# Moving VectorE work in a two-layer attention block: the gate's modulation, the query rotation, retention tiles and score maxima

## The chip, the cores and the metric

The kernel runs on one NeuronCore of a Trainium2 chip. The metric is the device time of one execution in microseconds. Five instruction streams work side by side and wait for each other through semaphores: TensorE (PE in the profile, with its weight loads as PEld), VectorE (DVE), ScalarE (ACT), GpSimd (POOL) and SyncE (SP), whose queue issues nearly all DMA transfers.

## The reference

Two layers over a sequence of 1024 tokens with 1024 features. Each layer normalizes x, scales and shifts it with a modulation computed from a condition vector c, projects it once, runs three kinds of attention on slices of that projection, gates each with a SiLU, projects back, and adds the result times a modulation gate:

```
shift, scale, gate = split(silu(c) @ ada_w[l] + ada_b[l], 3)
h = rms_norm(x, norm_w[l]) * (1 + scale) + shift
ret_p, mla_p, gla_p = split_cols(h @ w_in[l], ...)
r_o = rms_norm(retention(rope(rq), rope(rk), rv))        # 4 heads of 64, chunks of 64, decay
m_o = mla(mq, mkv, mkr, ...)                             # 8 heads, low-rank q and kv, softmax, causal by chunk
g_o = rms_norm(gla(gq, gk, gv, gg, ...)) * gla_norm      # 4 heads, gated linear attention, chunks of 64
x = x + gate * (concat(r_o*silu(rz), m_o*silu(mz), g_o*silu(gz)) @ w_out[l])
```

After two layers comes a final rms_norm. All is float32. In `mla` the queries are an up-projection of a rank-256 latent; 32 features per head are rotated by position (rope), 64 are not, and the softmax subtracts the row maximum of the scores.

## The kernel before

Features lie on the 128 partitions and tokens along the free dimension, in two halves of 512 (`hf`). A float32 product is made of three fast matmuls: each operand is split into a high and a low part, and `mm3` (L556, L557, L558) adds high by high, high by low, low by high in one PSUM bank. One projection of 128 output features over one half is 8 such triples, 24 matmuls of 128x512.

**Stages of a layer**, in PE's order: retention's queries and keys; the latents `mkv`, `mq0`, `mq1`; the retention values `rv` with features on the free side (`proj_v`, 8 groups of 128 tokens); the MLA keys (`mk`); `gq`; the rotated part of the MLA queries (`mla_queries` up to its `yield`); the gate projection `rz0`; the other MLA queries (`mla_queries` after the `yield`, tiles `mq`); `rz1`; `gk`; the values `gv` with GLA's preparation beside them; `gz0`, `gz1` with the GLA core; `mz0` to `mz3`; then the MLA heads and the output projection.

**What sets the order.** PE's order is written by hand: it is the program's order (`manual_schedule` for PE). Side work is put between the matmuls of the projections by `task` and `tick`: a task is a generator, each `tick` lowers its counter by one, and at zero one step of it is issued, which names the next distance. A projection ticks after each `mm3`, a `proj_v` after every second one. Three such tasks matter here. `ret_core` is retention tile by tile (128 tokens, 8 tiles): it starts `RW[0]` ticks after the MLA keys and spreads its tiles by `RW[1]`. `mla_max` computes 176 score tiles a layer only for their row maxima: a matmul (L1243) to a PSUM bank, and a DVE reduction (L1245) that frees it; it yields `MAXW` ticks between two of them, and its banks go round the tags in `self.maxp`. `head_out` normalizes a finished head pair, transposes it through PSUM (L874) and multiplies by the gate (L878, L880). What a task hasn't done at a `drain` is issued there at one go; the last maxima come out that way behind `mz3`, ahead of the MLA values `mv`. The orders of DVE, ACT, POOL and SP come from a scheduler with a model of time, which takes what is ready, earlier program text first; on the chip each of these engines runs its list strictly in that order.

**PSUM** has four tags of two buffers each: `pj`, `mm`, `s`, `acc`. From the MLA keys on, projections have only the two `pj` buffers, so the third one to come waits until an eviction has freed the first. Evictions are an ACT copy (L717, L1078, L694), or for the `mq` tiles an ACT copy to a high part and a DVE subtraction for the low part (`pair_out`, L1107), which frees the bank. The `s` and `mm` buffers carry retention's scores (L790, freed by DVE's decay multiplication L793), its state products (L802 freed by L804, L815 freed by L823 and L825) and the maxima.

**Modulation** (`ada`, L567-580) is no matmul: a chunk of 512 of its outputs streams 8 tiles of 256 KB through three SBUF buffers, and DVE multiplies each with a broadcast silu(c) and adds along the row (L576, 128x512 each, kept in program order). A layer's own chunks are `(l, 4)` and `(l, 5)`, the two halves of its gate, which are not used before the output projection; layer 0 also computes the four chunks of layer 1. `next_chunk(x)` is called at named points "a" to "o", and issues one chunk if x is in `CHUNKS`. Point "c" stands ahead of `proj_v` for `rv`, "e" behind `gq`, "f" behind `rz0`, "g" behind `rz1`.

**Query rotation** (`q_rope`): per half six DVE products and sums (L732 to L737) on two 128x512 tiles, two DVE casts to the high part (L1118), two POOL subtractions for the low part (L1119), and four DMAs to DRAM scratch (L1121).

## Time and profile before

| what | us |
|---|---|
| median of three runs | 1194.8 (1193.62 to 1195.11) |
| profiled execution | 1194.69 |
| its span (first to last instruction) | 1192.9 |
| PE busy | 1136.0 (95%) |
| PE weight loads busy | 947.2 (79%) |
| DVE busy | 787.9 (66%) |
| ACT busy | 595.6 (50%) |
| POOL busy | 529.5 (44%) |
| mean granted PE clock | 0.969 |

How to read it: the timeline view lists instructions of one engine with start and duration; consecutive ones of a line and shape are put together (x8), with the duration of all of them. What stands in brackets is the idle time of the engine before it, and the engine, tile and line that released it. The view by windows gives each engine's busy time in a stretch of the span, and in its column PEclk the mean granted clock of PE as a share of the full one. A `128x512` matmul starts 0.23 us after the one before it at full clock (397.19, 397.42 and 397.65 us on the timeline) and 0.43 us at half clock; its duration as listed is longer, since matmuls overlap.

### The profile page before, as it was taken

The page shows a single profiled execution, that of the slowest core. Times are in us where ns is not written, and L with a number is a line of the kernel's source. Part 1 is how long each engine was busy: PE and PEld are TensorE (multiplying, and loading weights), DVE is VectorE, ACT ScalarE, POOL GpSimd, SP SyncE. Part 2 cuts the span into 40 slices and gives each one's busy share as a digit, 9 for nine tenths or more (in the row PEclk, how much of TensorE's full clock was granted, in tenths as well). Part 3 has the DMA queues.
Part 4 walks back from the last instruction along what each step waited for, and adds up shares of the span by engine and source line. Part 5 has one row for each costly group of instructions (what it writes and reads, how often), then busy time and mean ns, then how long its engine had stood idle before and what let it go on. Part 6 is the DMA issues. An engine that isn't in the chain of part 4 may idle for free. (4 is left out here: it accounts for less than half of the span.)

```text
span 1192.9 us, 16951 instructions
## 1 busy us (share of the span) xinstructions
PE 1136.0 (95%) x5968; PEld 947.2 (79%) x5968; DVE 787.9 (66%) x1366; ACT 595.6 (50%) x1164; POOL 529.5 (44%) x459
## 2 busy tenths in 40 slices
PE   7999989899999899999999999789999989999996
PEld 4878967688877688888787898668888868888896
DVE  7864298568776656868875437863875565686754
ACT  6434432333554478863543443144355547886431
POOL 0064154245533346683565324424453334668630
PEclk8899998799999899999999999799999989999999
DMA  9816173672136634238453325536221663424722
GB/s 374 278 56 174 45 259 121 212 218 79 42 103 184 151 89 107 62 132 310 176 178 92 108 89 203 176 133 202 62 58 41 175 151 89 107 63 147 258 90 71
DMA packets 65585, 169.01 MB, mean 142 GB/s; under 512 B 10262, under 2 KB 13334, under 8 KB 65500
## 3 DMA queue, kind: packets, MB, share of 16 engines
q1 hardware_dynamic: 65500, 167.93, 45.0%
q8 instruction: 47, 0.77, 0.3%
q14 instruction: 38, 0.31, 0.1%
HBM read 125.36 MB, written 38.41 MB: 137 GB/s over the span
## 5 line engine op out<-in xcount | busy, mean ns | idle before, releaser
L457 POOL TENSOR_TENSOR wwo_wl<-wwo_wst,wwo_wh 128x1024 fp32r<-128x1024 f32 x27 | 69.1, 2563 | 38.9 <-ACT wwo_wh L456 38.9
L1269 POOL TENSOR_TENSOR mhead_wh<-mhead_p,mhead_wh 128x384 fp32r<-128x384 f32 (+1 forms) x48 | 57.9, 1206 | 56.9 <-DVE mhead_wh L1268 56.9
L576 DVE SCALAR_TENSOR_TENSOR ada_aw<-ada_aw,silrow 128x512 f32<-128x512 f32 x64 | 71.2, 1139 | 9.8 <-DMA ada_aw<-awc 9.5
L1245 DVE TENSOR_REDUCE mmax_mx<-mmax_psmm 128x1 f32<-128x512 f32 (+1 forms) x88 | 51.9, 590 | 22.0 <-PE mmax_psmm L1243 21.0
L1245 DVE TENSOR_REDUCE mmax_mx<-mmax_psacc 128x1 f32<-128x256 f32 (+2 forms) x88 | 45.5, 517 | 21.6 <-PE mmax_psacc L1243 20.4
L1274 DVE TENSOR_TENSOR mhead_ph<-mhead_pss,mhead_ph 128x512 fp32r<-128x512 f32 x48 | 33.0, 688 | 36.1 <-ACT mhead_pss L1273 36.1
L556 PE MATMUL pmz_pspj<-mkh_h,wmz_wh 128*128 128x512 f32 x128 | 52.5, 410 | 0.0
L1269 POOL TENSOR_TENSOR mhead_wl<-mhead_p,mhead_wl 128x128 fp32r<-128x128 f32 (+1 forms) x48 | 35.8, 746 | 34.8 <-DVE mhead_wl L1268 34.8
L557 PE MATMUL pmz_pspj<-mkh_h,wmz_wh 128*128 128x512 f32 x128 | 50.4, 394 | 0.0
L558 PE MATMUL pmz_pspj<-mkh_h,wmz_wl 128*128 128x512 f32 x128 | 50.1, 391 | 0.0
L558 PE MATMUL wo_pspj<-gran_mx,wwo_wl 128*128 128x512 f32 (+1 forms) x120 | 44.3, 369 | 1.7 <-POOL wwo_wl L457 1.7
L556 PE MATMUL wo_pss<-gran_mx,wwo_wh 128*128 128x512 f32 (+1 forms) x120 | 44.6, 371 | 0.0
L556 PE MATMUL wo_pspj<-gran_mx,wwo_wh 128*128 128x512 f32 (+1 forms) x120 | 44.5, 371 | 0.0
L558 PE MATMUL wo_pss<-gran_mx,wwo_wl 128*128 128x512 f32 (+1 forms) x120 | 44.1, 368 | 0.0
L557 PE MATMUL wo_pss<-gran_mx,wwo_wh 128*128 128x512 f32 (+1 forms) x120 | 44.1, 368 | 0.0
L557 PE MATMUL wo_pspj<-gran_mx,wwo_wh 128*128 128x512 f32 (+1 forms) x120 | 44.1, 368 | 0.0
L457 POOL TENSOR_TENSOR wrk_wl<-wrk_wst,wrk_wh 128x1024 fp32r<-128x1024 f32 x3 | 8.0, 2679 | 77.2 <-ACT wrk_wh L456 77.2
L600 ACT ACTIVATE ssq_sq<-ssq_x 128x512 f32<-128x512 f32 (+1 forms) x31 | 16.5, 534 | 51.3 <-DVE ssq_x L1371 51.3
L605 DVE TENSOR_TENSOR ssq_sq<-ssq_sq,ssq_sq 128x512 f32<-128x512 f32 (+1 forms) x30 | 30.2, 1006 | 13.9 <-ACT ssq_sq L600 13.8
L556 PE MATMUL pv_pspj<-wgv_wh,mkh_h 128*128 128x256 f32 x128 | 37.2, 291 | 0.4 <-ACT pv_v L694 0.3
L451 DVE SCALAR_TENSOR_TENSOR rstd_rt<-rstd_psmm,rstd_rt 128x512 f32<-128x512 f32 (+1 forms) x13 | 8.4, 650 | 43.9 <-ACT rstd_rt L447 43.9
L1272 ACT ACTIVATE mhead_ph<-mhead_pss 128x512 fp32r<-128x512 f32 x48 | 28.6, 596 | 17.2 <-PE mhead_pss L1262 16.6
(560 smaller groups left out, 4166.1 us busy)
## 6 DMA issues: line engine op xcount, KB each, us to landing
ada_aw<-awc SPq DMA_DIRECT2D x64, 256.0 KB
wwo_wst<-wo SPq DMA_DIRECT2D x32, 512.0 KB
aw<-awc SPq DMA_DIRECT2D x11, 512.0 KB
x<-xT SPq DMA_DIRECT2D x8, 512.0 KB
kn<-mk_ph SPq DMA_DIRECT2D x16, 256.0 KB
kn<-mk_pl SPq DMA_DIRECT2D x16, 256.0 KB
qn<-mq_ph SPq DMA_DIRECT2D x16, 256.0 KB
qn<-mq_pl SPq DMA_DIRECT2D x16, 256.0 KB
```

Source lines behind the costliest of these rows:

```text
L451: V.scalar_tensor_tensor(t, ss, d * EPS, t, ALU.add, ALU.mult)
L457: (eng or nc.gpsimd).tensor_tensor(lo, src, hi.bitcast(F32), ALU.subtract)
L556: mm(ps, lh, rh, start=start, stop=False)
L557: mm(ps, lh, rl, start=False, stop=False)
L558: self.last = mm(ps, ll, rh, start=False, stop=stop)
L576: step = nc.vector.scalar_tensor_tensor(v, v, 1.0, self.silrow[:, cs], ALU.mult, ALU.mult, accum_out=t[:, 2 * j + i:2 * j + i + 1])
L600: nc.scalar.activation(sq, self.x[k][:, cs], AF.Square)
L605: nc.vector.tensor_tensor(o[0], o[0], sq, ALU.add)
L1245: nc.vector.tensor_reduce(mx[:, i, j:j + 1], ps[:, :w], AX.X, ALU.max)
L1269: nc.gpsimd.tensor_tensor(pl, p, ph.bitcast(F32), ALU.subtract)
L1272: nc.scalar.activation(ph, s, AF.Exp, scale=ATT_SCALE)
L1274: nc.vector.tensor_tensor(pl, s, ph.bitcast(F32), ALU.subtract)
```

## The change

Five edits, which change no result. PE, ACT, POOL and SP issue the same work in another order, and DVE has two instructions fewer of 1205 rows.

1. `CHUNKS` goes from "efgkno" to "ccgkno", and `next_chunk` issues as many chunks as the letter occurs. The two gate chunks of each layer (16 L576 instructions and 16 DMAs a layer) are issued at "c", so they run under `rv`'s `proj_v` and not in the stage of the queries.
2. `RW` goes from (16, 4) to (18, 6): retention starts two ticks later, and its tiles stand six ticks apart.
3. `mla_queries` issues both halves' `q_rope` behind the `yield`, that is in program order behind `rz0`, and not ahead of it.
4. `MAXW` goes from 1.35 to 1.15: a score maximum every 1.15 ticks.
5. The maxima's banks are `mm` and `s` (four buffers) and not `mm`, `acc` and `s` (six) up to the GLA core; `mm` and `acc` during it, as before; and `mm` and `s` again behind it, where `acc` was kept.

```diff
-CHUNKS = "efgkno"
+CHUNKS = "ccgkno"
...
-MAXW = 1.35
-RW = (16, 4)
+MAXW = 1.15
+RW = (18, 6)
...
     def next_chunk(self, at):
-        if self.chunks and at in CHUNKS:
+        for _ in range(min(len(self.chunks), CHUNKS.count(at))):
             self.ada(*self.chunks.popleft())
...
+        x = [[], []]
         for hf in range(2):
-            x = []
             for i in range(2):
                 ps = self.ps("pj")
                 self.uq_mtile(w, ql, i, hf, ps)
-                x.append(self.pt(name="qx"))
-                nc.scalar.copy(x[i], ps)
-            self.q_rope(l, x, hf, *tab[hf])
-            self.lab = "mq_"
+                x[hf].append(self.pt(name="qx"))
+                nc.scalar.copy(x[hf][i], ps)
         yield
+        for hf in range(2):
+            self.q_rope(l, x[hf], hf, *tab[hf])
         self.lab = "mq_"
         for pr in range(4):
...
-        self.maxp = ("mm", "acc", "s")
+        self.maxp = ("mm", "s")
...
         mz = [self.proj_silu(l, "mz0")]
         self.drain(core)
+        self.maxp = ("mm", "s")
         self.next_chunk("l")
```

**DVE around the end of `rz0`.** In the kernel before, the rotation stands between retention tiles and L576 steps of the gate, ahead of `rz0`'s SiLU (L433); the first `mq` eviction (L1107) stands behind that SiLU and three L576 steps. Layer 0, before, the first half's rotation, with `ada_aw` the streamed modulation tile:

```order
L732 TENSOR_TENSOR mrope_ra_1567<-mq_qx_1565,pv_tab_1269 128x512
L733 TENSOR_TENSOR mrope_rb_1568<-mq_qx_1525,pv_tab_1269 128x512
L736 TENSOR_TENSOR mq_qx_1565<-mq_qx_1565,pv_tab_1268 128x512
L576 SCALAR_TENSOR_TENSOR ada_aw_1507,ada_sm_1485<-ada_aw_1507,silrow 128x512
L734 TENSOR_TENSOR mq_qx_1525<-mq_qx_1525,pv_tab_1268 128x512
L737 TENSOR_TENSOR mq_qx_1565<-mq_qx_1565,mrope_rb_1568 128x512
```

Now, behind the SiLU of `rz0`'s second half; the six sums and two casts of the first half, then those of the second, follow each other, and the first `mq` eviction stands last:

```order
L433 SCALAR_TENSOR_TENSOR prz_zu_1757<-mq_rz_319_1612,prz_zt_1756 128x512
L732 TENSOR_TENSOR mrope_ra_1764<-mq_qx_1561,pv_tab_1323 128x512
...
L1118 CAST mrope_qrh_1778<-mq_qx_1561 128x512
L732 TENSOR_TENSOR mrope_ra_1784<-mq_qx_1610,pv_tab_1323 128x512
...
L1118 CAST mrope_qrh_1798<-mq_qx_1610 128x512
L793 TENSOR_TENSOR retc_ram_1817<-retc_pss_1811,cst 128x2x128
L793 TENSOR_TENSOR retc_ram_1817<-retc_pss_1812,cst 128x2x128
L804 TENSOR_TENSOR retc_rks_1826<-retc_psmm_1823,cst 128x256
L862 TENSOR_REDUCE hnorm_sm_1845<-hnorm_hsq_1843 128x8
L1107 TENSOR_TENSOR mq_pl_1856<-mq_pspj_1804,mq_ph_1855 128x512
```

All sixteen DVE instructions of the rotation moved to between `rz0`'s second SiLU and the first `mq` eviction. On PE, two `mq` tiles and one retention tile stand between `rz0` and the third `mq` tile, which needs the bank that this eviction frees.

**PE behind `mz3`.** Here the maxima left over are issued at one go (`mv` is the first matmul of the next stage). Before, 20 of them and one L1215; the first and the last two:

```order
L1243 MATMUL mmax_psmm_3815<-mmax_mxk_2241,mmax_mxq_2240 128x512
L1243 MATMUL mmax_psacc_3818<-mmax_mxk_2241,mmax_mxq_2240 128x128
...
L1215 MATMUL mmax_psmm_3849<-cst,mmax_sm_3847 8x128
...
L1243 MATMUL mmax_psmm_3878<-mmax_mxk_2243,mmax_mxq_2242 128x512
L1243 MATMUL mmax_psacc_3881<-mmax_mxk_2243,mmax_mxq_2242 128x512
L556 MATMUL mv_pspj_3894<-wukvv_wh_3639,pmz_lat_3528 128x256
```

Now 10, on `mm` and `s`, and no L1215 among them:

```order
L1243 MATMUL mmax_psmm_3854<-mmax_mxk_2243,mmax_mxq_2242 128x384
L1243 MATMUL mmax_pss_3857<-mmax_mxk_2243,mmax_mxq_2242 128x512
...
L1243 MATMUL mmax_psmm_3878<-mmax_mxk_2243,mmax_mxq_2242 128x512
L1243 MATMUL mmax_pss_3881<-mmax_mxk_2243,mmax_mxq_2242 128x512
L556 MATMUL mv_pspj_3894<-wukvv_wh_3676,pmz_lat_3556 128x256
```

The other ten, and the L1215 with the sums of a finished group, moved forward into the projections.

**DVE beside GLA's preparation.** While `gv` runs on PE, DVE's list now has, in layer 0, one stretch of GLA preparation without a reduction of maxima (the L913 is a scan over 256 columns, issued twice):

```order
L1245 TENSOR_REDUCE mmax_mx_2434<-mmax_pss_2453 128x1
L913 SCALAR_TENSOR_TENSOR glap_gt_2388<-reset,glap_gz_2387 128x256 x2
L916 TENSOR_TENSOR glap_gel_2389<-glap_gt_2388 128x512
L928 TENSOR_TENSOR glap_gea_2346<-glap_gea_2346 128x4
L929 TENSOR_TENSOR glap_gqb_2337<-pgq_gq_1488,glap_gz_2387 128x256
L939 TENSOR_TENSOR glap_gkp_2333<-pgk_gk_2254,glap_gz_2387 64x8x64 x2
L930 TENSOR_TENSOR glap_gkm_2331<-pgk_gk_2254,glap_gel_2389 128x4x64
L931 TENSOR_TENSOR glap_gkm_2331<-pgk_gk_2254,glap_gt_2388 128x4x64
L935 TENSOR_TENSOR glap_gka_2335<-pgk_gk_2254,glap_gt_2388 64x4x64 x2
L942 TENSOR_TENSOR glap_gkl_2332<-pgk_gk_2254,glap_gel_2389 128x4x64
L423 SCALAR_TENSOR_TENSOR glap_gt_2459<-glap_gz_2458 128x512
L1245 TENSOR_REDUCE mmax_mx_2434<-mmax_psmm_2531 128x1
```

On PE, 66 matmuls (columns of 256) stand between the maximum `mmax_pss_2453` and `mmax_psmm_2569`, whose buffer the last reduction shown frees. In the kernel before, the same stretch of DVE had two reductions between its steps, and six buffers took the maxima.

## The prediction

> **What bounds the kernel now.** I read the page's engine shares first, then PE's waits, the view by windows, and last the timelines of the stages that these point to. The profiled execution took 1194.69 us, 0.1 below the median of the runs; its span is 1192.9 us and 1.8 us lie around it. My sum goes against 1194.7.

> ```profile
> PE 1136.0 (95%) x5968; PEld 947.2 (79%) x5968; DVE 787.9 (66%) x1366; ACT 595.6 (50%) x1164; POOL 529.5 (44%) x459
> ```

> PE is the bound, with 56.9 us idle over the span. The change gives it no instruction less, so it can only win what PE waits, or what it runs at less than full clock. The waits:

> ```profile
> PE mq_pspj L556 <- DVE mq_pl L1107: 8.5, 7, 2.2
> PE retc_pss L790 <- DVE retc_ram L793: 5.7, 4, 1.9
> PE mmax_psmm L1215 <- DVE mmax_sm L1211: 4.0, 2, 2.0
> PE retc_psmm L815 <- DVE pgq_rst L823: 3.8, 2, 1.9
> PE mmax_psacc L1243 <- DVE pv_gz L880: 2.6, 1, 2.6
> PE prz_pspj L556 <- ACT mq_qx L1078: 1.9, 2, 0.9
> ```

> Four of the six belong to the stage from `gq` to `rz1`, where retention's first tiles, the rotation and the gate's modulation all want DVE: 8.5 + 5.7 + 3.8 + 1.9 = 19.9 us over both layers. The other two belong to the maxima. The windows show what comes with them:

> ```profile
> 120.00:140.00 20.00, 20.00 (x138) 18.99 (x138) 8.30 (x11) 8.73 (x21) 3.35 (x3) 1.00 0.22 67
> 160.00:180.00 20.00, 16.13 (x93) 12.91 (x91) 18.54 (x34) 4.75 (x7) 9.82 (x6) 0.93 0.64 214
> 180.00:200.00 20.00, 17.67 (x94) 14.46 (x94) 18.57 (x45) 5.04 (x12) 10.70 (x13) 0.82 0.47 171
> 200.00:220.00 20.00, 17.49 (x113) 13.96 (x112) 13.56 (x39) 8.90 (x22) 6.04 (x9) 0.95 0.23 76
> 220.00:240.00 20.00, 19.44 (x68) 15.25 (x67) 8.51 (x20) 5.47 (x12) 6.99 (x9) 0.71 0.74 243
> 400.00:420.00 20.00, 17.01 (x74) 13.06 (x74) 15.98 (x33) 9.02 (x18) 6.38 (x13) 0.83 0.41 89
> 740.00:760.00 20.00, 15.38 (x77) 12.46 (x76) 18.70 (x42) 5.24 (x9) 7.89 (x5) 0.76 0.53 168
> 760.00:780.00 20.00, 18.42 (x111) 15.35 (x110) 15.82 (x39) 5.63 (x15) 11.95 (x14) 0.90 0.28 106
> ```

> Columns: window, its length, then PE, PEld, DVE, ACT, POOL busy, granted clock, DMA share, GB/s. From 160 to 200 DVE is busy 18.5 of 20 us and PE is not; in the second 20 us window of layer 1 that shows it, 740 to 760, the same. The granted clock is below 1 in just these windows: what PE loses to it is (1 − clock) times its busy time, 0.07 x 16.13 + 0.18 x 17.67 + 0.05 x 17.49 + 0.29 x 19.44 = 10.8 us in layer 0 and 0.24 x 15.38 + 0.10 x 18.42 = 5.5 us in layer 1. The query stage therefore loses 19.9 + 16.3 = 36.2 us in both layers, 3% of the kernel. Under the values, 120 to 140, DVE is busy 8.3 of 20 us.

> **The gate's modulation under the values.** I cost it at nothing where it goes.

> ```profile
> L576 DVE SCALAR_TENSOR_TENSOR ada_aw<-ada_aw,silrow 128x512 f32<-128x512 f32 x64 | 71.2, 1139 | 9.8 <-DMA ada_aw<-awc 9.5
> 149.19 0.69 DVE L1107 TENSOR_TENSOR mk_pl<-mk_pspj,mk_ph 128x512 fp32r<-128x512 f32 x1 [12.78 <-ACT mk_ph L1106]
> ```

> Sixteen steps a layer at 1.14 us are 18.2 us of DVE. It is free for 11.7 us of 120 to 140, and then to 149.19: 20.9 us in all, so they fit, narrowly, and PE's matmuls for the values hide them. What they can hold up is the normalization of the latents on the same DVE, since a step in the list waits for its DMA (9.5 us of such waits in the group). Three steps are in flight at a time, 3 x 1.14 = 3.4 us: the term lies between 0 and 3.4 us of loss a layer. A gain here is excluded; what it frees is counted in the next term.

> **The query stage.** Without the gate's steps and the rotation in it, and with tiles six ticks apart, I take the waits ahead of `rz0`'s end and behind it, with their half clock, as gone: 36.2 us fall away. One new wait comes: all of the rotation now stands on DVE between `rz0`'s second SiLU and the first `mq` eviction, and PE wants the bank of that eviction for the third `mq` tile. Rows for both sides:

> ```profile
> 239.92 0.59 ACT L717 COPY mq_rz<-prz_pspj 128x512 f32<-128x512 f32 x1 [4.22 <-PE prz_pspj L558]
> 243.26 0.63 ACT L434 ACTIVATE prz_zu<-prz_zu 128x512 f32<-128x512 f32 x1 [0.76 <-DVE prz_zu L433]
> 181.94 0.69 DVE L734 TENSOR_TENSOR mq_qx<-mq_qx,pv_tab 128x512 f32<-128x512 f32 x1
> 182.54 0.68 DVE L737 TENSOR_TENSOR mq_qx<-mq_qx,mrope_rb 128x512 f32<-128x512 f32 x1
> 187.64 1.30 DVE L732 TENSOR_TENSOR mrope_ra<-mq_qx,pv_tab 128x512 f32<-128x512 f32 x1
> 189.73 0.94 DVE L736 TENSOR_TENSOR mq_qx<-mq_qx,pv_tab 128x512 f32<-128x512 f32 x1
> 185.25 0.76 DVE L1118 CAST mrope_qrh<-mq_qx 128x512 fp32r<-128x512 f32 x2
> 192.66 1.49 DVE L1118 CAST mrope_qrh<-mq_qx 128x512 fp32r<-128x512 f32 x2
> 194.07 0.74 DVE L793 TENSOR_TENSOR retc_ram<-retc_pss,cst 128x256 f32<-128x256 f32 x2
> 194.73 0.41 DVE L804 TENSOR_TENSOR retc_rks<-retc_psmm,cst 128x256 f32<-128x256 f32 x1
> 195.06 1.21 DVE L825 SCALAR_TENSOR_TENSOR pgq_rst<-pgq_rst,cst,retc_psmm 64x64 f32<-64x64 f32 x4
> 216.15 0.69 DVE L1107 TENSOR_TENSOR mq_pl<-mq_pspj,mq_ph 128x512 fp32r<-128x512 f32 x1
> 206.66 0.71 PE L790 MATMUL retc_pss<-prk_rh,prk_rh 64*128 64x128 f32 x8
> 209.28 0.48 PE L556 MATMUL mq_pspj<-latn_lat,wuq_wh 128*128 128x512 f32 x1
> ```

> DVE's side, counted from `rz0`'s last matmul: the SiLU's DVE step is done 3.3 us later (copy at 239.92, the step that follows it at 243.26). Then twelve products and sums 0.60 us apart (182.54 behind 181.94) are 7.2, two pairs of casts at 0.76 are 1.5, the state update between them 1.2, and 0.74 + 0.41 of the tile, a head's reduction of about the eviction's size and the eviction itself (0.69) 2.5: 15.7 us. The same forms also took 0.94 to 1.30, and a pair of casts 1.49 (187.64, 189.73, 192.66); with the casts and two sums so, it is 17.8. PE's side: an `mq` tile, six matmuls 0.23 us apart, 1.4; a retention tile, 209.28 − 206.66 = 2.6; another `mq` tile, 1.4: 5.4 us. So PE waits 10.3 to 12.4 us, and I take 10.7, near the lower end, since POOL and ACT here mostly wait for the rotation themselves. Behind such a wait the clock is down: the stretch 400 to 420, with one gap of 2 us in it (quoted below), lost 0.17 x 17.01 = 2.9 us by it. I take 2.6 for that, and 1.5 for small waits behind it, of the two 2.2 us waits that L1107 has at most today: 14.8 us a layer, 29.6 in both. The stage gains 36.2 − 29.6 = **6.6 us**.

> **The maxima**, three terms, from these rows:

> ```profile
> 399.15 0.40 PE L1243 MATMUL mmax_psmm<-mmax_mxk,mmax_mxq 104*128 104x512 f32 x1
> 404.92 0.39 PE L1215 MATMUL mmax_psmm<-cst,mmax_sm 128*8 128x128 f32 x2 [2.02 <-DVE mmax_sm L1211]
> 409.33 0.42 PE L556 MATMUL mv_pspj<-wukvv_wh,pmz_lat 128*128 128x256 f32 x1
> 255.85 0.39 PE L1243 MATMUL mmax_psacc<-mmax_mxk,mmax_mxq 104*128 104x256 f32 x1 [1.02 <-DVE mq_rz L878]
> 359.57 0.50 PE L1243 MATMUL mmax_psacc<-mmax_mxk,mmax_mxq 104*128 104x512 f32 x1 [2.57 <-DVE pv_gz L880]
> 280.06 0.28 PE L558 MATMUL pv_pspj<-wgv_wh,mkh_h 128*128 128x256 f32 x1
> 280.18 0.40 PE L1243 MATMUL mmax_psacc<-mmax_mxk,mmax_mxq 104*128 104x512 f32 x1
> 286.02 0.69 DVE L1245 TENSOR_REDUCE mmax_mx<-mmax_psacc 128x1 f32<-128x512 f32 x1
> ```

> The leftover behind `mz3`: 20 maxima took 409.33 − 399.15 = 10.2 us, 0.51 apiece, DVE's pace. Now 10 are left: 5.1 us. The 2.9 us of low clock in that window mostly go too, since the wait at 404.92 is not among them any more; against that the ten that moved and L1215 cost PE ten times at most 0.23 us where they go. 5.1 + 2.3 − 2.3 = 5.1, and I take 4.9 a layer, **9.8 us**; between 5.1 − 2.3 = 2.8 and 7.4 a layer.

> The `acc` bank: the two waits of maxima behind `head_out`, 1.02 and 2.57, are layer 0's alone, and go with the bank: **3.6 us**; between 2.6 (the longer one only) and 3.6.

> GLA's preparation pays. A reduction there ran 286.02 − 280.18 = 5.8 us behind its matmul and nothing waited, because six buffers at 1.35 ticks hold 8.1 ticks, and a tick is six matmuls of 0.12 us (280.06 to 280.18), 0.7 us: 5.8. Four buffers at 1.15 hold 4.6 ticks, 3.3 us. The same lag stalls PE 2.5 us, and the three more maxima that the denser spacing puts here cost DVE 0.51 each: 4.0 in layer 0; layer 1 I take at 2.5, its end without the added maxima. Loss **6.5 us**; between 2.5 (one lag in all) and, with two lags in each layer and half clock behind each like the 2.9 us above, 4 x (2.5 + 2.9) = 21.6.

> [...]

> **The sum.** 6.6 + 9.8 + 3.6 − 6.5 = 13.5 us; 1194.7 − 13.5 = **1181 us**.

> **The rivals.** *The rotation is slower than its best rows.* If DVE shares the stretch with POOL's low parts and waits for their DMAs, all sixteen steps run at the slow rows: 12 x 0.94 + 2 x 1.49 = 14.3 in place of 8.7, 21.3 us behind `rz0` and not 15.7, and the tile's steps behind a transfer. At 5 us more a wait of 15.9; each further `mq` tile then waits its 2.2 us (six left), and the clock stays low for them. That is 15.9 + 2.9 + 6 = 24.8 a layer, 49.6 against 36.2: the stage loses 13.4 us, which with 9.8 + 3.6 − 6.5 makes 1201. The point from which it decides against the change is 21.5 us lost a layer, that is a wait of 17. For it: 187.64 and 192.66; against it: the other rows, and that the gate's steps, which stood between, are gone. *The half clock isn't the stalls' work* and stays: then 16.3 us of the 36.2 don't fall away, and the time is 1197; only the place of the clock's windows speaks against it. *The leftover only moves*: maxima at 1.15 stall the projections for what the shorter leftover saves, 1181 + 9.8 = 1191. DVE's share under `mz` speaks against it, the group's 0.51 apiece for it. *The new wait is short*: if the list's model is right that the rotation is through earlier, 5 us of wait and no low clock, it is 1181 − 2 x (5.7 + 2.6) = 1164. *The modulation is in the way under the values*: 3.4 us a layer, 1188.

> **How the numbers follow.** The forecast has 0.48, the slow rotation 0.16, the half clock that stays 0.05, the leftover that moves 0.11, the short wait 0.12, the modulation 0.08. This kernel's runs tell 0.2%, 2.4 us, from no change. Faster: the forecast, the short wait, most of the leftover and of the modulation, and the slow rotation's mild end: 0.73. Within 0.2%: 0.10, where mishaps just balance; slower: 0.17. The range of 8 in 10 leaves out most of the short wait at its low end, and the worst of the slow rotation: 1168 to 1200. The likeliest case alone, by the bounds of its terms, is 1172 to 1190.

> **What would show it.** Right: a profile without the waits on `retc_ram`, `pgq_rst` and `mq_qx`; a clock near 1 from 160 to 190; one wait of 10 to 12 us a layer of `mq_pspj` on `mq_pl`, low clock behind it; 5 us between `mz3` and `mv`; no wait of `mmax` on L878 or L880; small waits of `mmax` on L1245 beside `gv`. Wrong: a wait of `mq_pspj` under 6 or over 15 us; a low clock in 160 to 190 without waits; waits of maxima in the `gz` and `mz` projections; `rv` or the keys waiting for the latents.

## The result, and the profile after

The changed kernel takes 1183.85 us (median of four runs, 1180.76 to 1186.4) against 1194.45 of the kernel before: a ratio of 0.991, 95% interval 0.9886 to 0.9935. Its profiled execution took 1183.94 us with a span of 1182.2. The page's engine shares and PE's waits:

```profile
PE 1118.6 (95%) x5968; PEld 933.9 (79%) x5968; DVE 785.9 (66%) x1366; ACT 596.2 (50%) x1164; POOL 525.8 (44%) x459
```

```profile
PE mq_pspj L556 <- DVE mq_pl L1107: 25.6, 4, 12.5
...
PE mmax_psmm L1215 <- DVE mmax_sm L1211: 3.7, 3, 2.1
PE mv_pspj L556 <- DVE pmz_vl L1189: 3.1, 2, 1.5
...
PE prz_pspj L556 <- DVE mq_pl L1107: 2.3, 2, 1.2
...
PE mmax_psmm L1243 <- DVE mmax_mx L1245: 1.5, 5, 0.7
```

DVE ran 1366 instructions in both profiled executions, so the two that the section on the change counts as fewer are not missing. The waits on `retc_ram`, `pgq_rst` and `mq_qx` are no longer in the list, nor is that of the maxima on `pv_gz`. In their place stands one kind of wait of 25.6 us, nearly all of it in two pieces of 12.5 us, one a layer. The windows, with the columns of those above:

```profile
120.00:140.00 20.00, 20.00 (x135) 18.92 (x135) 13.88 (x36) 8.12 (x19) 3.13 (x3) 1.00 0.73 229
160.00:180.00 20.00, 20.00 (x112) 16.08 (x110) 11.76 (x20) 5.82 (x9) 11.22 (x9) 1.00 0.63 223
180.00:200.00 20.00, 17.61 (x117) 14.61 (x114) 11.93 (x29) 8.19 (x17) 5.22 (x5) 1.00 0.00 1
200.00:220.00 20.00, 9.59 (x46) 7.53 (x47) 14.48 (x29) 4.45 (x10) 9.16 (x11) 0.66 0.49 190
400.00:420.00 20.00, 17.90 (x101) 14.88 (x101) 14.72 (x29) 14.16 (x29) 10.21 (x16) 1.00 0.36 84
760.00:780.00 20.00, 7.47 (x43) 5.84 (x43) 16.11 (x29) 5.90 (x12) 8.78 (x8) 0.77 0.33 126
```

Under the values (120 to 140) DVE now has 13.9 us of work and PE loses nothing. From 160 to 180 PE is full and at full clock. From 200 to 220 it is busy 9.6 of 20 us.

The view by tile gives the first and last start of a group of instructions, and so the length of each stage. In layer 0 of the changed kernel:

```profile
L556 PE MATMUL pgq_pspj<-mkh_h,wgq_wh x16: 387/389/390, 155.5 to 165.8; 128*128 128x512 f32 x16
L556 PE MATMUL pgk_pspj<-mkh_h,wgk_wh x16: 389/398/478, 243.0 to 256.2; 128*128 128x512 f32 x16
L557 PE MATMUL pmz_pspj<-mkh_h,wmz_wh x64: 387/395/628, 340.3 to 400.2; 128*128 128x512 f32 x64
L556 PE MATMUL mv_pspj<-wukvv_wh,pmz_lat x16: 277/283/385, 404.3 to 438.8; 128*128 128x256 f32 x16
```

Taken with the last L558 of each tile, the same view of each kernel that follows gives the table below, in us; each row is one profiled execution, its time the median of the runs. The columns are the query stage from the last matmul of `gq` to the first of `gk`; the middle from there to the last of `mz3`; the leftover from there to the first of `mv`; and where `gq` starts in layer 0.

| kernel | time | query stage, layer 0, 1 | middle | leftover | `gq` starts |
|---|---|---|---|---|---|
| before | 1194.45 | 81.4, 79.8 | 153.7, 148.9 | 10.4, 10.9 | 153.2 |
| changed | 1183.85 | 76.8, 76.9 | 157.4, 152.4 | 3.9, 3.9 | 155.5 |
| gate chunks alone | 1173.51 | 68.3, 69.4 | 154.5, 148.9 | 10.9, 10.9 | 153.7 |
| RW alone | 1195.51 | 79.5, 79.1 | 154.7, 148.9 | 10.8, 10.5 | 153.8 |
| chunks and RW | 1171.96 | 67.1, 68.8 | 154.7, 149.0 | 10.8, 10.6 | 154.1 |
| rotation alone | 1215.65 | 89.1, 90.4 | 153.4, 149.0 | 10.8, 10.9 | 151.8 |
| MAXW alone | 1188.74 | 79.7, 80.9 | 156.6, 152.5 | 3.8, 3.9 | 153.9 |
| banks alone | 1197.85 | 78.2, 80.9 | 155.4, 151.5 | 10.9, 10.9 | 154.2 |
| MAXW and banks | 1185.73 | 78.2, 78.5 | 155.4, 152.4 | 3.9, 3.9 | 154.2 |
| changed, rotation back | 1161.97 | 66.8, 67.0 | 155.7, 152.4 | 3.9, 3.9 | 153.9 |
| changed, half the rotation back | 1173.13 | 72.6, 72.2 | 156.9, 152.4 | 3.9, 4.0 | 154.5 |
| changed, rotation behind `mq` | 1178.5 | 75.7, 76.1 | 156.9, 152.4 | 3.9, 3.9 | 152.3 |

Between before and changed the query stages gain 7.5 us, the leftovers 13.5, and the middles lose 7.2: 13.8 us. The two profiled executions differ by 10.8; 2.3 of the rest lie ahead of `gq`, whose start varies from 151.8 to 155.5 in this table, also among kernels with the same program up to point "c". They lie ahead of `rv` already, whose first matmul starts at 118.14 us before and at 120.49 now.

### The profile page after: what moved, and what is told of

Same layout as the page of the kernel before. It is cut to its first block, busy times and chain, and to the rows that moved or that the text cites. A ratio compares the mean times of both kernels' runs of the same rounds, so it can differ in the third digit from the quotient of the medians.

```text
span 1182.2 us, 16973 instructions
## 1 busy us (share of the span) xinstructions
PE 1118.6 (95%) x5968; PEld 933.9 (79%) x5968; DVE 785.9 (66%) x1366; ACT 596.2 (50%) x1164; POOL 525.8 (44%) x459
## 4 chain that ended last, share of the span: by engine, by line
PE 75%; DVE 12%; DMA 5%; ACT 4%; issue 3%; POOL 1%; SPq 0%; DVEq 0%; POOLq 0%; ACTq 0%
PE mhead_psacc L1294 3%; PE mhead_psacc L1292 3%; PE mhead_psacc L1293 3%; PE pmz_pspj L556 3%; PE pmz_pspj L557 2%; PE pmz_pspj L558 2%; DMA ada_aw<-awc 2%; DVE mmax_mx L1245 2%; PE wo_pss L558 2%; PE wo_pspj L556 2%; PE wo_pss L556 2%; PE wo_pss L557 2%; PE wo_pspj L558 2%; PE wo_pspj L557 2%; PE mhead_pss L1260 2%
## 5 line engine op out<-in xcount | busy, mean ns | idle before, releaser
L457 POOL TENSOR_TENSOR wwo_wl<-wwo_wst,wwo_wh 128x1024 fp32r<-128x1024 f32 x27 | 69.4, 2575 | 39.0 <-ACT wwo_wh L456 38.9
L1245 DVE TENSOR_REDUCE mmax_mx<-mmax_psmm 128x1 f32<-128x512 f32 (+1 forms) x96 | 57.4, 598 | 34.9 <-PE mmax_psmm L1243 33.9
L576 DVE SCALAR_TENSOR_TENSOR ada_aw<-ada_aw,silrow 128x512 f32<-128x512 f32 x64 | 60.6, 966 | 18.6 <-DMA ada_aw<-awc 18.4
L1274 DVE TENSOR_TENSOR mhead_ph<-mhead_pss,mhead_ph 128x512 fp32r<-128x512 f32 x48 | 33.0, 688 | 36.2 <-ACT mhead_pss L1273 35.7
L556 PE MATMUL pmz_pspj<-mkh_h,wmz_wh 128*128 128x512 f32 x128 | 53.3, 417 | 0.0
L558 PE MATMUL pmz_pspj<-mkh_h,wmz_wl 128*128 128x512 f32 x128 | 50.6, 395 | 0.0
L556 PE MATMUL mq_pspj<-latn_lat,wuq_wh 128*128 128x512 f32 x48 | 21.6, 450 | 26.0 <-DVE mq_pl L1107 25.6
L558 PE MATMUL wo_pspj<-gran_mx,wwo_wl 128*128 128x512 f32 (+1 forms) x120 | 44.3, 369 | 1.9 <-POOL wwo_wl L457 1.9
L556 PE MATMUL wo_pss<-gran_mx,wwo_wh 128*128 128x512 f32 (+1 forms) x120 | 44.5, 371 | 0.0
L556 PE MATMUL wo_pspj<-gran_mx,wwo_wh 128*128 128x512 f32 (+1 forms) x120 | 44.5, 371 | 0.0
L558 PE MATMUL wo_pss<-gran_mx,wwo_wl 128*128 128x512 f32 (+1 forms) x120 | 44.1, 368 | 0.0
L457 POOL TENSOR_TENSOR wrk_wl<-wrk_wst,wrk_wh 128x1024 fp32r<-128x1024 f32 x3 | 8.0, 2682 | 79.5 <-ACT wrk_wh L456 79.5
L1272 ACT ACTIVATE mhead_ph<-mhead_pss 128x512 fp32r<-128x512 f32 x48 | 28.6, 596 | 17.8 <-PE mhead_pss L1262 17.3
L1243 PE MATMUL mmax_psmm<-mmax_mxk,mmax_mxq 104*128 104x512 f32 (+1 forms) x96 | 35.5, 370 | 2.0 <-DVE mmax_mx L1245 1.5
L556 PE MATMUL pv_pspj<-wgv_wh,mkh_h 128*128 128x256 f32 x128 | 37.0, 289 | 0.0
```

The costliest lines, as they stand in the source:

```text
L457: (eng or nc.gpsimd).tensor_tensor(lo, src, hi.bitcast(F32), ALU.subtract)
L556: mm(ps, lh, rh, start=start, stop=False)
L558: self.last = mm(ps, ll, rh, start=False, stop=stop)
L576: step = nc.vector.scalar_tensor_tensor(v, v, 1.0, self.silrow[:, cs], ALU.mult, ALU.mult, accum_out=t[:, 2 * j + i:2 * j + i + 1])
L1243: nc.tensor.matmul(ps[:, :w], st["q"][0:104, 128 * i:128 * i + 128], st["k"][0:104, 512 * j:512 * j + w], start=True, stop=True)
L1245: nc.vector.tensor_reduce(mx[:, i, j:j + 1], ps[:, :w], AX.X, ALU.max)
```

## The experiments

Each was timed beside the kernel before on the same chip, which there had medians of 1195.6 to 1196.4; ratios are to that.

**The rotation back ahead of the yield, all else as changed.**

```diff
...
         for hf in range(2):
+            x = []
...
+            self.q_rope(l, x, hf, *tab[hf])
+            self.lab = "mq_"
         yield
-        for hf in range(2):
-            self.q_rope(l, x[hf], hf, *tab[hf])
```

> The change without its third edit: the rotation issued ahead of the yield again, all else as changed. Theory: the rotation's place alone makes the one wait of 12.5 us a layer of the third mq tile, the waits of 0.3 and 1.2 us behind it and the half clock there (about 17 us a layer, 34 in both), and under tiles six ticks apart and without the gate's steps the rotation fits beside rz0 with at most 2 us of waits a layer: 1150 to 1156 us, clock 1.0 from 160 to 220. Rival: the rotation was itself what crowded VectorE in the kernel before; waits on retc_ram, pgq_rst and mq_qx come back with half clock, 10 us or more a layer: 1170 us or more.

Measured: 1161.97 us, ratio 0.9725 (0.9705 to 0.9746), 22 us less than the change. The query stage falls by 10 us in each layer. On its timeline PE's waits in the query stage of layer 0:

```profile
179.28 0.90 PE L790 MATMUL retc_pss<-prk_rh,prk_rh 64*128 64x128 f32 x7 [1.32 <-DVE retc_ram L793]
182.44 0.49 PE L834 MATMUL retc_psacc<-mq_rst,retc_rqs 128*128 128x128 f32 x2 [0.49 <-POOL retc_rqs L798]
183.30 0.49 PE L834 MATMUL retc_psacc<-mq_rst,retc_rqs 128*128 128x128 f32 x2 [0.37 <-POOL retc_rqs L798]
200.53 0.50 PE L556 MATMUL mq_pspj<-latn_lat,wuq_wh 128*128 128x512 f32 x1 [1.51 <-DVE mq_pl L1107]
208.04 0.50 PE L556 MATMUL mq_pspj<-latn_lat,wuq_wh 128*128 128x512 f32 x1 [0.28 <-DVE mq_pl L1107]
216.42 0.51 PE L556 MATMUL prz_pspj<-mkh_h,wrz_wh 128*128 128x512 f32 x1 [1.17 <-DVE mq_pl L1107]
```

5.1 us of waits in place of the crowd, and the clock is 1.00 over the whole stage (its window is shown with the account of the prediction). The result lies between the two forecasts, 6 us above the theory's range, since 1.5 of the 12.5 us wait stays and 2.2 us of waits come ahead of `rz0`, but the rival's crowd does not come back: the rotation fits beside `rz0` once the gate's steps are gone, and its move is the part of the change that costs.

**The gate chunks and the tile spacing, each and together, on the kernel before.**

```diff
-CHUNKS = "efgkno"
+CHUNKS = "ccgkno"
...
-RW = (16, 4)
+RW = (18, 6)
```

With the first of them goes the loop in `next_chunk`, as in the change.

> The kernel before with the two gate chunks under the values and RW (18, 6), the rotation and the maxima as before. Theory: these two edits alone take away nearly all of the 36.2 us that the query stage loses: 1194.7 - 36.2 + 2 to 5 = 1161 to 1164 us. Rival: the rotation move is needed for it, and without it half of the loss stays: 1175 us or more.

> The kernel before with the two gate chunks under the values as the only edit. Both chunks and tile spacing together gave 1172 us on a kernel of 1195.6 (-23.7). Theory: the gate's steps are most of what crowds VectorE in the query stage (18 us of its work a layer), so this edit alone gives more than half of it: 1175 to 1183 us, with the waits on retc_ram and pgq_rst from tiles four ticks apart partly left. Rival: the spacing of the tiles is what counts and this edit gives under 5 us: 1190 us or more.

> The kernel before with RW (18, 6) as the only edit. Theory: with the gate's steps still in the stage VectorE is full from 160 to 200 whatever the spacing, and the tiles moved later meet the mq evictions: 1184 to 1193 us. Rival: the spacing is what counts: 1180 us or less.

Measured: together 1171.96 us, ratio 0.9811 (0.9787 to 0.9835); chunks alone 1173.51, 0.9805 (0.9788 to 0.9823); spacing alone 1195.51, 0.9995 (0.9976 to 1.0013). All of the gain is the chunks'. Alone they come out 1.5 us below the range expected of them, and the spacing alone 2.5 us above its own. The spacing alone turns several waits into fewer and longer ones; the first in layer 0, with the gate's steps still on DVE:

```profile
185.19 1.52 PE L790 MATMUL retc_pss<-prk_rh,prk_rh 64*128 64x128 f32 x8 [7.34 <-DVE retc_ram L793]
```

The theory of the first run expected 1161 to 1164 and got 1172: of the 36.2 us about 25 go (stages of 67.1 and 68.8 against 81.4 and 79.8), not 33. What is left in its list are small waits: 3.9 us on `mq_pl`, 2.8 on `retc_ram`, 2.3 of `prz_pspj` and 1.7 of `retc_psacc`, 10.7 over both layers. No run removes them.

**The rotation's move alone, on the kernel before** (the edit of `mla_queries` in the diff above, nothing else).

> The kernel before with the rotation behind the yield as the only edit. Theory: it takes the waits ahead of rz0's end (about 6 us a layer and part of the half clock) and adds the wait of 12 us or more with its half clock, and three steps of the gate stand between as well: 1196 to 1206 us. Rival: taking the rotation out of the crowded stretch is worth more than the new wait: 1190 us or less.

Measured: 1215.65 us, ratio 1.0172 (1.0149 to 1.0194), slower than expected. PE's longest wait:

```profile
PE mq_pspj L556 <- DVE mq_pl L1107: 38.9, 4, 18.4
```

18.4 us a layer and not 12.5: the gate's steps stand in the same block. The move costs 20 us on the kernel before and 22 us on the changed one. It never paid.

**Half of the rotation behind the yield.**

```diff
                 nc.scalar.copy(x[hf][i], ps)
+            if hf == 0:
+                self.q_rope(l, x[0], 0, *tab[0])
+                self.lab = "mq_"
         yield
-        for hf in range(2):
-            self.q_rope(l, x[hf], hf, *tab[hf])
+        self.q_rope(l, x[1], 1, *tab[1])
```

> The change with only the second half's rotation behind the yield; the first half's stays ahead of it, as in the kernel before. Theory: what PE waits for at the third mq tile is the length of VectorE's block between rz0's SiLU and the first mq eviction; half of the rotation shortens it by six sums at 0.60 and a pair of casts at 0.76, 4.4 us, to 5 us if the slower forms count: a wait of 7.5 to 8.1 us a layer in place of 12.5, and 1172 to 1177 us. Rival: the wait comes from the transfers of the low parts or from ScalarE and not from VectorE's length: it stays above 10 us, 1180 us or more.

Measured: 1173.13 us, ratio 0.9813 (0.9792 to 0.9833). The wait at the third `mq` tile in layer 0, the same in layer 1 (in this kernel L1109 is L1107 of the others):

```profile
204.26 0.79 PE L556 MATMUL mq_pspj<-latn_lat,wuq_wh 128*128 128x512 f32 x1 [5.96 <-DVE mq_pl L1109]
```

The wait goes 12.5, 6.0, 1.5 us with two, one and no halves of the rotation behind the yield, and the time 1183.9, 1173.1, 1162.0. It follows the length of DVE's block. The half that left was worth 6.6 us, more than the 4.4 to 5 expected; an estimate of the difference is in the next section.

**The rotation behind the eight `mq` tiles**, where no `mq` eviction can wait for it.

```diff
         yield
-        for hf in range(2):
-            self.q_rope(l, x[hf], hf, *tab[hf])
         self.lab = "mq_"
         for pr in range(4):
             ...
                 self.pair_out(self.qn[l], pr, hf, ps)
+        for hf in range(2):
+            self.q_rope(l, x[hf], hf, *tab[hf])
```

> The change with the rotation issued behind the eight mq tiles, so that on VectorE it stands behind their evictions and beside rz1. Theory: the 12.5 us wait is only that the list of VectorE has the rotation ahead of the first mq eviction; placed behind the last one it hides under rz1, and the result is the change less 34 us plus 1 to 4 us of small waits: 1150 to 1156 us, better than the rotation ahead of the yield (1162). Rival: the rotated rows now come late for the first maxima, which read them back through DMA, or rz1's SiLU and head_out wait behind it on VectorE: 1162 us or more.

Measured: 1178.5 us, ratio 0.984 (0.9815 to 0.9865): a miss. Nothing came late for the maxima; the block stopped the next thing on DVE's list. DVE's timeline from the rotation's first product, and PE's wait:

```profile
212.95 2.30 DVE L732 TENSOR_TENSOR mrope_ra<-mq_qx,pv_tab 128x512 f32<-128x512 f32 x1 [0.31 <-DMA qn<-mq_ph]
...
227.08 0.76 DVE L1118 CAST mrope_qrh<-mq_qx 128x512 fp32r<-128x512 f32 x2
227.87 0.76 DVE L793 TENSOR_TENSOR retc_ram<-retc_pss,cst 128x256 f32<-128x256 f32 x2
```

```profile
228.44 1.94 PE L830 MATMUL retc_psacc<-pv_v,retc_ram 128*128 128x64 f32 x8 [6.62 <-ACT prz_zt L431]
```

A retention tile beside `rz1` needs its decay multiplication (L793), which stands behind 14.9 us that are nearly all rotation. The releaser named is ACT, but the matmul reads `retc_ram`, which DVE finishes at 228.6, while PE begins on its first half. The wait moved from a projection to a retention tile and shrank from 12.5 to 6.6 us. The time fell by 5 us only: behind the wait the matmuls run at half clock up to 237.3 us, for 8.9 us (the eight L830 take 1.94 us, and 1.00 at 216.22), where behind the longer wait of the changed kernel they did so for some 4 (the last section sets the two side by side).

**The maxima: distance and banks, each and together, on the kernel before.**

```diff
-MAXW = 1.35
+MAXW = 1.15
...
-        self.maxp = ("mm", "acc", "s")
+        self.maxp = ("mm", "s")
...
         self.drain(core)
+        self.maxp = ("mm", "s")
         self.next_chunk("l")
```

> The kernel before with MAXW 1.15 and the new banks as the only edits. Theory: the leftover behind mz3 halves (5 us a layer), the acc waits go (3.6 us), new waits beside gv and gz cost 3 to 6 us: 1184 to 1189 us. Rival: what the leftover saves only moves into waits of the projections, and nothing or under 3 us is left: 1192 us or more.

> The kernel before with MAXW 1.15 as the only edit, the maxima still on three tags. MAXW and banks together gave 9.9 us. Theory: the shorter leftover behind mz3 is this edit's alone (6 us a layer with its low clock), and with six buffers there is next to no wait beside gv; the acc waits behind head_out stay or grow a little, 3 to 5 us: 1184 to 1189 us. Rival: denser maxima meet head_out on acc in both layers and give back most of it: 1190 us or more.

> The kernel before with the maxima's banks changed as the only edit, MAXW at 1.35. MAXW alone gave 7.7 us, both together 9.9. Theory: the waits behind head_out go (3.6 us in layer 0), four buffers cost little beside gv, and the leftover behind mz3 keeps its 10 us: 1190 to 1194 us. Rival: four buffers stall PE beside gv by more than that: no gain, 1195 us or more.

Measured: together 1185.73 us, ratio 0.9928 (0.9902 to 0.9953); MAXW alone 1188.74, 0.9933 (0.9916 to 0.995); banks alone 1197.85, 1.0026 (1.0006 to 1.0046). The shorter leftover is MAXW's. The banks alone do not gain: the theory that expected 1190 to 1194 fell. Without `acc`, at the old distance, PE waits beside `gv` in both layers:

```profile
285.95 0.50 PE L1243 MATMUL mmax_psmm<-mmax_mxk,mmax_mxq 104*128 104x512 f32 x1 [1.58 <-DVE mmax_mx L1245]
```

With MAXW 1.15 these are 0.2 to 0.7 us (in the changed kernel's list above: 1.5 us in five waits, the leftover's among them). So the two edits meet: the same four buffers cost less where the maxima fall on other places of DVE's list; the next section shows where.

**Two values tuned on the best version** (rotation back): MAXW 1.0, and RW (16, 5).

```diff
-MAXW = 1.15
+MAXW = 1.0
```

> The change with the rotation back ahead of the yield (1162 us) and MAXW 1.0 in place of 1.15. Theory: the leftover behind mz3 (3.7 us for ten maxima in the changed kernel) goes, its maxima cost PE 0.2 us each in the projections, and beside gv VectorE is full: the small waits there grow by 1 to 3 us a layer; together 1159 to 1163 us. Rival: VectorE cannot follow at one maximum a tick and waits of maxima appear in every projection: 1166 us or more.

```diff
-RW = (18, 6)
+RW = (16, 5)
```

> The change with the rotation back ahead of the yield (1162 us) and RW (16, 5) in place of (18, 6). Theory: without the gate's steps the spacing of the tiles counts for little either way (it alone gave nothing, and 1.5 us on top of the chunks): 1159 to 1165 us. Rival: six ticks are needed for the tiles to pass beside the rotation: 1167 us or more.

Measured: 1164.94 us, ratio 0.9751 (0.9731 to 0.9771), 2 us above the theory's range and not told apart from 1161.97: the leftover falls from 3.9 to 0.2 us a layer and the middle grows by 3.0 and 3.3. And 1171.86, ratio 0.9797 (0.9774 to 0.982), 10 us slower than with (18, 6): a miss. Its longest wait in layer 0 is on POOL:

```profile
184.78 1.66 PE L834 MATMUL retc_psacc<-pgq_rst,retc_rqs 128*128 128x128 f32 x4 [3.24 <-POOL retc_rqs L798]
```

Five ticks from the 16th put the second tile where the rotation stands: POOL scales the tile's queries (L798) only when it is through with two low parts of the rotation and a weight's low part between them, at 183.82 us. So the place of the tiles does count, and that RW alone gave nothing on the kernel before says little about it.

The fastest version is the change without its third edit, 1162 us: 2.7% under the kernel before and 1.9% under the change (0.9725 / 0.991).

## Why the prediction was right

The forecast was 1181 us, a gain of 13.5, the result 1183.85, a gain of 10.6, for mostly the reasons given. Two terms of the maxima were wrong and cancelled in part, and so did two sizes within the query stage: that the sum came out this near is in part luck.

**The gate's modulation under the values: right.** It costs nothing where it goes: from the first matmul of `rv` to the first of `gq` it is 35.0 us in each layer of both kernels (118.14 to 153.17 us before, 120.49 to 155.52 now, in layer 0), and PE is busy 20.00 of 20 us from 120 to 140.

**The query stage: right in sum, 7.5 us where 6.6 was forecast.** The crowd ahead of `rz0`'s end left as stated. Layer 0's stage as one window, with the columns of those above, in the kernel before, the changed one, and the one with the rotation back:

```profile
163.84:245.16 81.32, 72.05 (x369) 57.67 (x367) 56.12 (x131) 26.58 (x55) 33.20 (x37) 0.85 0.53 171
166.21:243.01 76.80, 62.82 (x369) 51.15 (x367) 43.10 (x95) 27.07 (x55) 31.11 (x37) 0.91 0.42 138
164.60:231.43 66.83, 61.69 (x369) 50.12 (x367) 46.16 (x95) 26.75 (x55) 32.23 (x37) 1.00 0.50 159
```

With the rotation back PE works for 61.7 us at full clock. Against that the kernel before loses 19.6 us in layer 0 and 18.1 in layer 1, 37.7 where 36.2 was counted, and the changed one 15.1 in each, 30.3 where 29.6 was. So both sides of this term hold. Within the second side two sizes cancel: the wait is longer than taken, and what lies behind it is some 3 us a layer (half clock and small waits) where 4.1 was taken.

The new wait was worked out as 10.3 to 12.4 us, 10.7 taken; it is 12.5. Both sides can be checked, ACT, DVE and POOL first, then PE:

```profile
192.09 0.59 ACT L717 COPY mq_rz<-prz_pspj 128x512 f32<-128x512 f32 x1 [2.38 <-PE prz_pspj L558]
```

```profile
195.30 0.68 DVE L732 TENSOR_TENSOR mrope_ra<-mq_qx,pv_tab 128x512 f32<-128x512 f32 x1
...
200.47 0.76 DVE L1118 CAST mrope_qrh<-mq_qx 128x512 fp32r<-128x512 f32 x2
201.15 1.75 DVE L732 TENSOR_TENSOR mrope_ra<-mq_qx,pv_tab 128x512 f32<-128x512 f32 x1
202.82 1.74 DVE L733 TENSOR_TENSOR mrope_rb<-mq_qx,pv_tab 128x512 f32<-128x512 f32 x1
204.49 0.68 DVE L736 TENSOR_TENSOR mq_qx<-mq_qx,pv_tab 128x512 f32<-128x512 f32 x1
...
209.40 1.28 DVE L1107 TENSOR_TENSOR mq_pl<-mq_pspj,mq_ph 128x512 fp32r<-128x512 f32 x2
```

```profile
201.04 2.97 POOL L1119 TENSOR_TENSOR mrope_qrl<-mq_qx,mrope_qrh 128x512 fp32r<-128x512 f32 x2 [3.31 <-DVE mrope_qrh L1118]
```

```profile
210.13 0.80 PE L556 MATMUL mq_pspj<-latn_lat,wuq_wh 128*128 128x512 f32 x1 [12.53 <-DVE mq_pl L1107]
...
211.15 0.63 PE L558 MATMUL mq_pspj<-latn_lat,wuq_wl 128*128 128x512 f32 x1
211.58 0.63 PE L556 MATMUL mq_pspj<-latn_lat,wuq_wh 128*128 128x512 f32 x1
```

From the ACT copy to the eviction's end DVE's side took about 18 us, forecast 15.7 to 17.8; PE's side 197.6 − 192.1 = 5.5, forecast 5.4. The difference on DVE is two products of 1.75 us and not 0.60, just while POOL takes the first half's low parts (201.04, 2.97 us): 2.3 us. The step that was mis-sized is the choice of the lower end "since POOL and ACT here mostly wait for the rotation themselves". They wait for its first half, and POOL then works beside its second. If this overlap goes with the half that was issued ahead, that half's 4.4 us and these 2.3 make 6.7, an estimate near the 6.6 that it was worth. The whole trace of the changed kernel, where L732 to L737 also serve retention's queries and keys, shows slow products in the same company: of their 56 single products and sums of 128x512, the 35 that share at most 0.2 us with work of POOL take 0.68 or 0.69 us, and 18 of the 21 others 1.74 to 2.88. No run here varies that alone, so that POOL's work is the cause is not shown. The half clock behind the wait came nearly as forecast: matmuls 0.43 us apart from 210.13 for some 4 us, a loss of 2 us where 2.6 was taken.

**The rival of the slow rotation** thus had its place right, beside POOL's low parts, and its size wrong: two of twelve products were slow (1.75 us each), not all. Alone on the kernel before, where the gate's steps join the block, the wait passes the 17 us that the prediction named as the point of decision: 18.4 us, and 1215.65. That the half clock stays, and that the wait is short, were refuted by the windows and by 12.5 us. That the clock is down behind a wait of 10 us the prediction took from a gap of 2 us: its rows hold no wait of PE above 2.57 us. The first to show it is the changed kernel's 200 to 220, with 0.66 at the wait of 12.5 us.

**The maxima: 6.9 us forecast, 6.3 by the table, with two terms wrong.** The leftover gains 13.5 us, 6.8 a layer, where 5.1 and 2.3 were added up. That sum counted part of the low clock twice: the 10.2 us of the 20 maxima already hold the wait of 2.02 us and the slow matmuls behind it, so 0.51 apiece is not the maxima's own pace; the ten that remain take 3.65 us (400.67 to 404.32), 0.37 apiece. Of the gain the maxima that moved take some back in the middle: layer 1, which had no `acc` waits, shows the price plainly, 3.5 us longer. Less 0.75 us of new waits, this is 2.7 us for ten maxima and one L1215, where 2.3 was taken. Net of that the leftover gives 8.1, forecast 9.8. GLA's preparation was forecast to lose 6.5 us and the waits beside `gv` add some 2 (1.7 against 0.5 before in layer 0, 1.0 against 0.2 in layer 1). The step that failed is "a tick is six matmuls of 0.12 us". It leaves out the maximum itself:

```profile
267.27 0.28 PE L1243 MATMUL mmax_pss<-mmax_mxk,mmax_mxq 104*128 104x256 f32 x1
...
273.45 0.34 PE L1243 MATMUL mmax_psmm<-mmax_mxk,mmax_mxq 104*128 104x384 f32 x1
274.34 0.40 PE L1243 MATMUL mmax_pss<-mmax_mxk,mmax_mxq 104*128 104x512 f32 x1
275.28 0.40 PE L1243 MATMUL mmax_psmm<-mmax_mxk,mmax_mxq 104*128 104x512 f32 x1
```

```profile
267.59 0.42 DVE L1245 TENSOR_REDUCE mmax_mx<-mmax_pss 128x1 f32<-128x256 f32 x1
...
276.78 0.55 DVE L1245 TENSOR_REDUCE mmax_mx<-mmax_psmm 128x1 f32<-128x384 f32 x1
```

One maximum and six matmuls take 0.94 us, so four buffers cover more than the 3.3 us used. And the forecast did not see a pause: where a group of maxima ends, the code holds the next one back for some six ticks (the close of the group yields four, and `MAXW` stands ahead and behind), so PE asks for no buffer from 267.27 to 273.45, just while DVE works off the stretch without a reduction (267.9 to 276.8). That they meet is luck of the new distance. With the banks alone, at the old distance, the pause lies from 271.35 to 277.00, and the wait of 1.58 us comes in the second stretch of GLA's steps, behind it.

**The `acc` bank: 3.6 us forecast, next to nothing left.** Its waits went as stated, but another took their place in the same stretch of layer 0:

```profile
347.27 0.39 PE L1215 MATMUL mmax_psmm<-cst,mmax_sm 128*8 128x128 f32 x2 [2.09 <-DVE mmax_sm L1211]
```

It comes with MAXW, not with the banks (the run of MAXW alone has it with 2.09 us too, that of the banks alone does not): at the new distance a group's end meets that place. It stands in `mz0`, where the prediction had named a wait of maxima as a sign against it. Nor do both old waits go with the bank alone: in the run of MAXW alone, which keeps `acc`, the one of 2.57 us is gone and the one of 1.02 is left. Here a wait that was taken away was replaced by the next one on DVE's list; the forecast asked what is late next for the rotation and did not for the maxima.

## What to carry to other kernels

On an engine that runs its list in order, the length of the uninterrupted block ahead of what another engine waits for is what counts: two, one and no halves of the rotation in it made PE wait 12.5, 6.0 and 1.5 us. A long piece of work without a deadline (here the rotation, 12 to 15 us as a block) belongs where the waiting engine needs nothing from that list for as long. Cutting it up finer than by halves was not tried. An edit that is argued together with others must be run without each of them: here one of the five cost 22 us, about what another one had earned, and the sum still came out ahead. A buffer count is judged by the time between two uses, counted with all instructions in between, and by the place of the owner's long steps, not by the mean distance.

## What the runs showed of the hardware that was not expected

A short wait does not always bring the half clock. The kernel before has waits of 1.99, 0.52 and 0.54 us at its `mq` tiles of layer 0 and a granted clock of 0.95 and 0.71 in 200 to 220 and 220 to 240. The run of both maxima edits has waits of 1.98, 0.89, 0.36 and 2.01 us at the same tiles and a clock of 1.00 in both windows:

```profile
217.91 0.50 PE L556 MATMUL mq_pspj<-latn_lat,wuq_wh 128*128 128x512 f32 x1 [1.98 <-DVE mq_pl L1107]
...
227.48 0.50 PE L556 MATMUL mq_pspj<-latn_lat,wuq_wh 128*128 128x512 f32 x1 [2.01 <-DVE mq_pl L1107]
```

```profile
214.59:218.00 3.41, 1.42 (x8) 1.05 (x8) 3.36 (x8) 0.86 (x2) 0.97 (x1) 1.00 0.65 179
218.00:231.65 13.65, 12.58 (x36) 9.41 (x35) 8.39 (x24) 3.85 (x9) 3.29 (x6) 0.50 0.80 263
```

```profile
222.97:226.39 3.42, 2.14 (x10) 1.34 (x9) 2.27 (x7) 2.21 (x5) 0.41 (x2) 1.00 0.77 255
226.39:229.80 3.41, 2.32 (x10) 1.95 (x11) 1.98 (x9) 1.16 (x4) 1.05 (x1) 1.00 0.88 258
229.80:233.21 3.41, 3.37 (x16) 2.38 (x14) 1.71 (x3) 1.54 (x3) 0.00 (x0) 1.00 1.00 383
```

Before, the whole gap of 1.99 us lies in one window, and the four that follow, 13.65 us, run at half clock. In the other run an edge cuts the gap of 2.01 us ahead of 227.48 in two, and the clock stays. In the traces of the kernel before and the changed one, over the same stretch, six such windows at full clock had 1.99 to 3.41 us without PE work, and half clock followed each. It also followed three with 1.58, 1.79 and 1.79 us, and did not follow seven others with 1.52 to 1.85, nor any with less. The place on the same edges also goes with what a long wait costs behind it: of the 13.65 us at half clock that go with the wait of 12.5 us (200.78 to 214.43), PE spent 9.35 waiting, but of the 10.24 us (227.10 to 237.34) that go with the wait of 6.6 us only some 1.3. No run moves the edges alone against one kernel, so that the place is the cause is not shown, and waits longer than 3.41 us had half clock behind them wherever they fell: those of 12.5, 6.6 and 6.0 us, the last with a clock of 0.83 in 200 to 220.
